# TensorE in tracing order in the stage of the last layer's first token group of a hybrid Conformer / RWKV-7 step

## The chip, the cores and the metric

The kernel runs on one core of a Trainium2 chip, as one launch. The metric is the device time of one execution in microseconds (us). The engines are called as the profile calls them: PE is TensorE's matmuls (PEld its weight loads), DVE is VectorE, ACT is ScalarE, POOL is GpSimd, SP is SyncE, which issues most DMAs.

## The reference

One inference step of a decoder of two layers with 1024 features, for a prompt of 1024 tokens (behind 16 learned meta tokens) and 8 single decode tokens, 1048 rows in all. Layer 0 mixes tokens with a causal Conformer convolution, layer 1 with RWKV-7; each is followed by a squared-ReLU MLP of width 4096. All is fp32. What matters here is the second half of layer 1:

```python
def _wkv7_step(S, inp):                       # per head, a 64x64 state
    r_t, w_t, k_t, v_t, kk_t, a_t = inp
    sa = einsum('bhvk,bhk->bhv', S, -kk_t)
    S = S * w_t + sa * (kk_t * a_t) + v_t * k_t
    return S, einsum('bhvk,bhk->bhv', S, r_t)
...
    yn = group_norm(y) * gn_g + gn_b          # per head, over 64 channels
    out = ((yn + bonus) * g) @ w_o            # "z" is (yn + bonus) * g
...
    h = h + out
    h = h + square(relu(rmsnorm(h) @ w_mlp_in)) @ w_mlp_out
```

## The kernel before

Every fp32 product of two big matrices is done as three fp32r matmuls: weights and activations are split into a rounded part (`_hi`) and a rest (`_lo`), and `mm3` (L187, L188, L189) adds hi·hi, lo·hi and hi·lo in PSUM. These are called **dense matmuls** below: 128x128 weights against 328 or 352 tokens. ACT casts the weights' hi part (L157), POOL subtracts for the lo part (L162), and DVE and ACT split the activations (L140, L141). `dense()` makes one 128-feature output tile of 24 dense matmuls and calls `fill()` in its middle, so that the work is cut into pieces of 12; `out` of the MLP calls `fill()` after every 6.

The rows are worked through in three token groups of 328, 352 and 352 for the output projection (`mixer_out`, tiles `ps_oo`, with eight inputs `zr` loaded from DRAM by SP at L1488 and split to `z_h`, `z_l`) and the MLP (`mlp`, tiles `ps_in` and `out`). The stage of this change is that of the first group. Before its start the projections of layer 1 (`p_v` the last of them, with `vt`, `nn` and `pk` behind them) have been done for all tokens.

Beside the dense work runs the recurrence, in 17 chunks of 64 tokens one after the other. `chunk()` is a generator. One chunk issues on PE: `A` (L1209, eight matmuls), `gg` (L1247), `bT` (L1270, eight transposes), `W` (L1277), `po` (L1247), `U` (L1293), `S` (L1302), `Y` (L1309 and L1312). A block of gg, po, W, U or S is 16 small matmuls on 32x32 or 64-wide parts of the array, one of Y 32; the trace has two records for each of these and for each matmul of A. Between them stand evictions on ACT and DVE, and each of them uses one of three PSUM banks (tag "w"). The last chunk's state goes out through `pfs` (L1330). At the stage's start the first twelve chunks are done. Two other streams run beside it: `decode_step` (L1368 to L1399, one step of the recurrence for the 8 decode tokens, `Sdec`) and `norm_gate`, which makes z for the later token groups, a half of the heads at a time: load of `ey`, mean and square, `yn` (four transposes on PE, L1429), `ez` (ACT, L1433), two DVE operations (L1435, L1436), a store to `d_z` by SP (L1437). The square `eq` (L1417) of the next half lies in the same buffer as `ez`, so it waits until that store has landed; behind it come L1422 to L1425 on DVE and ACT, and the next `yn`.

`filler()` deals these streams out over the stage's `fill()` calls, by the paces FA for the recurrence and NGA for decode and norm gates. This is the order of tracing. It isn't the order in which the engines run: the whole kernel is built under a scheduler that orders every engine's instructions from a timeline model of its own. So before the change the pieces of the three streams stand on PE where that planner puts them. Each engine then works its list strictly in order.

Lines of the stage: the `with` that is added stands round L1563 to L1566 (before). What follows is the stage of the second group.

Of the kernel before, what the change touches and what calls it, by code (L numbers as in the profile page):

```python
# [48 lines left out]
def hybrid_step(tc, x_prompt, x_sample, state_conv, state_shift, state_wkv, meta_tokens,  # L49
# [8 lines left out]
    nc = tc.nc  # L58
    ctx = ExitStack()
    with ctx:  # L60
# [77 lines left out]
        def split(hi, lo, src, eng_lo):  # L138

            nc.scalar.copy(hi, src)  # L140
            eng_lo.tensor_sub(lo, src, hi.bitcast(F32))  # L141
# [7 lines left out]
        def load_w(src, shape, name, eng_lo, tag="w", raw=None):  # L149

            a, b = shape
            if raw is None:
                raw = load_raw(src, shape, name)
            nb = cur["bufs"][tag]
            hi = cur["wsp"].tile([P, 8 * P], F32R, name=f"{name}_hi", tag=tag + "h", bufs=nb)
            lo = cur["wsp"].tile([P, 8 * P], F32R, name=f"{name}_lo", tag=tag + "l", bufs=nb)
            nc.scalar.copy(hi[:, :a * b], raw[:, :a * b])  # L157

            step = 2 * P if eng_lo is nc.gpsimd else a * b
            for c in range(0, a * b, step):  # L160
                cs = slice(c, min(c + step, a * b))
                eng_lo.tensor_sub(lo[:, cs], raw[:, cs], hi[:, cs].bitcast(F32))  # L162
            v = lambda t: t[:, :a * b].rearrange("p (a b) -> p a b", a=a)
            return v(hi), v(lo)
# [5 lines left out]
        def load_col(w, m, name, eng_lo, tag="w"):  # L170
            return load_w(col_src(w, m), (KT, P), name, eng_lo, tag)
# [13 lines left out]
        def mm3(ps, w, act, first, last):  # L185

            nc.tensor.matmul(ps, w[0], act[0], start=first, stop=False)  # L187
            nc.tensor.matmul(ps, w[1], act[0], start=False, stop=False)  # L188
            nc.tensor.matmul(ps, w[0], act[1], start=False, stop=last)  # L189

        def bank(name, tag="mm"):
            return cur[tag].tile([P, 512], F32, name=name, tag=tag)

        def dense(w, act, n, name, fill=None):
            ps = bank(f"ps_{name}")
            for k in range(KT):
                mm3(ps[:, :n], (w[0][:, k, :], w[1][:, k, :]), (act[0][:, k, :n], act[1][:, k, :n]), k == 0, k == KT - 1)
                if fill and k == KT // 2 - 1:
                    fill()
            return ps  # L200
# [5 lines left out]
        def tt(name, tag):  # L206
            return cur["tmp"].tile([P, cur["n"]], F32, name=name, tag=tag)
# [95 lines left out]
        def mlp(layer, groups, lag, eng_w, eng_h, fill=None, done=None):  # L303


            w_in, w_out = w_mlp_in[layer], w_mlp_out[layer]
            nj = DFF // P
            hid = {}

            def load_in(j):  # L310
                return load_col(w_in, j, f"wi{layer}_{groups[0][0]}_{j}", eng_w)

            def load_out(b):

                for i in range(2):
                    src = w_out[2 * b * P:(2 * b + 2) * P, i * 4 * P:(i + 1) * 4 * P].rearrange("(j p) c -> p j c", p=P)
                    yield load_w(src, (2, 4 * P), f"wo{layer}_{groups[0][0]}_{b}_{i}", eng_w)

            def inp(j, w, group):
                gn, hv, n, ah, al, rs, hid_pool = group  # L320
                if j % 2 == 0:
                    hid[gn, j // 2] = [hid_pool.tile([P, 2, cur["wide"]], F32R, name=f"h{q}{layer}{gn}_{j}", tag=f"h{q}") for q in "hl"]
                hh, hl = hid[gn, j // 2]
                ps = dense(w, (ah, al), n, f"in{layer}_{j}_{gn}", fill)
                with tc.high_priority(offset=HR):
                    r = tt(f"r{layer}_{j}_{gn}", "t1")
                    nc.vector.scalar_tensor_tensor(r[:, :n], ps[:, :n], 0.0, rs[:, :n], op0=ALU.max, op1=ALU.mult)  # L327
                    s = tt(f"s{layer}_{j}_{gn}", "t2")
                    nc.scalar.activation(s[:, :n], r[:, :n], AF.Square)  # L329
                    split(hh[:, j % 2, :n], hl[:, j % 2, :n], s[:, :n], eng_h)  # L330

            def out(b, i, w, group):
                gn, hv, n, ah, al, rs, hid_pool = group
                hh, hl = hid[gn, b]
                for m in range(4):
                    ps = bank(f"out{layer}_{b}_{gn}_{4 * i + m}")
                    for j in range(2):
                        mm3(ps[:, :n], [part[:, j, m * P:(m + 1) * P] for part in w], (hh[:, j, :n], hl[:, j, :n]), j == 0, j == 1)
                    with tc.high_priority(offset=HA):
                        nc.vector.tensor_add(hv[:, 4 * i + m, :], hv[:, 4 * i + m, :], ps[:, :n])  # L340
                    if fill:
                        fill()

            def outs(b):
                for i, w in enumerate(load_out(b)):
                    for group in groups:
                        out(b, i, w, group)

            last = nj - 1
            for j in range(last):  # L350
                w = load_in(j)
                for group in groups:
                    inp(j, w, group)
                b, odd = divmod(j - lag, 2)
                if b >= 0 and odd:
                    outs(b)
                if fill:
                    fill()
            for b in range((last - lag) // 2, nj // 2 - 1):
                outs(b)  # L360
            w, wo = load_in(last), list(load_out(nj // 2 - 1))
            for group in groups:
                inp(last, w, group)
                for i in range(2):
                    out(nj // 2 - 1, i, wo[i], group)
                if done and group is not groups[-1]:
                    done(group[0])

        with ExitStack() as l0:
# [6 lines left out]
            actp = [pool(l0, f"actp0{i}", 1) for i in range(2)]  # L376
            residp = [pool(l0, "resid00", 1)]
# [253 lines left out]
            with ExitStack() as s:  # L631
# [3 lines left out]
                fill, rest = filler(8 * KT, ([ranked(CV0, conv(0)), ranked(CV0, ln_silu(0))], EARLY * (15 * KT // 2 + 2 + 2 * MW + KT)))  # L635
# [43 lines left out]
            hidp = pool(l0, "hidp0", 2)  # L679
# [790 lines left out]
        with ExitStack() as l1:  # L1470
            open_weights(l1, 5, {"w": 5}, "f")
            open_tmp(l1, N2, "2", 3)
            residp = pool(l1, "resid1", 1)
            actp = pool(l1, "actp1", 1)
            hidp = pool(l1, "hidp1", 2)
# [5 lines left out]
            def mixer_out(g, residp, actp, fill, add):  # L1481
                lo, n = G2[g]
                h1 = hl[g] = residp.tile([P, KT, cur["wide"]], F32, name=f"h1_{g}", tag="h")
                nc.sync.dma_start(h1[:, :, :n], d_h[:, :, lo:lo + n])
                z = new_act(actp, f"z{g}", cur["wide"])
                for p in range(KT):
                    t = tt(f"zr{g}{p}", "t1")
                    nc.sync.dma_start(t[:, :n], d_z[:, p, lo:lo + n])  # L1488
                    split(z[0][:, p, :n], z[1][:, p, :n], t[:, :n], nc.vector)
                for m in range(KT):  # L1490
                    ps = dense(load_col(rwkv_w_o[0], m, f"wo{g}_{m}", nc.gpsimd), z, n, f"oo{g}_{m}", fill)
                    nc.vector.tensor_add(h1[:, m, :n], h1[:, m, :n], ps[:, :n])
                    add(m, h1[:, m, :n])
                    fill()
# [57 lines left out]
            def group(g, actp, hidp, sums):  # L1552
                n = G2[g][1]
                hv = hl[g][:, :, :n]
                return (g, hv, n, *mlp_in(actp, hv, n, 1, f"m1{g}", sums), hidp)
# [3 lines left out]
            fill, rest = filler(2 * KT + MLP_POINTS,  # L1559
                                ([until(NCH - 1)], FA * CHUNK_WAIT * (NCH - 1 - st["done"])),  # L1560
                                ([decode_step(), norm_gates(GN_OF[1]), ng2], NGA))
            add, sums = sums_of(0)
            mixer_out(0, residp, actp, fill, add)  # L1563
            mlp(1, [group(0, actp, hidp, sums)], 2, nc.gpsimd, nc.vector, fill)
            for _ in rest:
                pass  # L1566
            lw.close()
            outp = pool(l1, "outp", 1)
            cur["wide"] = max(n for lo, n in G2[1:])
# [2 lines left out]
            fill, rest = filler(2 * KT, ([ng2], NGB))  # L1572
            add, sums = sums_of(1)
# [6 lines left out]
            fill, rest = filler(2 * KT + MLP2_POINTS, ([ranked(FN, final(0))], FB))  # L1580
            add, sums = sums_of(2)
# [3 lines left out]
            def done(g):  # L1585
                end.append(filler(KT, ([final(g)], 24)))
# [38 lines left out]
```

## Time and profile before

| | |
|---|---|
| median of 3 runs | 2855.38 us (2850.13 to 2861.68) |
| span of the profiled execution | 2857.3 us |
| PE busy | 2677.4 us, 94% of the span |
| DVE, POOL, ACT busy | 69%, 60%, 47% |
| the stage | from the last projection (about 1837 us) to the second group's first `ps_oo` (2276.4 us) |
| the stage, PE and DVE busy | 413.65 us and 312.83 us of 440 |

The profiled execution has no time of its own beside its span of 2857.3 us; that lies 1.9 us over the median and within the three runs. PE is the engine that bounds the kernel nearly everywhere, and the profile's PE row says little about how well it is used: the ends of matmuls are modelled and overlap (a dense matmul of 328 columns has 0.31 us in the records and the next starts 0.15 us later). So in this stage the starts of matmuls are to be read, not their busy time.

### The profile page before, as it was taken

Reading aid. Unit: us, or ns where it says so; the run is one execution under the profiler, and the core shown is the slowest. Engines: PE = TensorE matmul, PEld = TensorE weight load, DVE = VectorE, ACT = ScalarE, POOL = GpSimd, SP = SyncE. Lnnn points to the kernel's source line nnn. Section 1 sums busy time; section 2 is a strip of 40 time slices with the busy share of each in tenths; the row PEclk is TensorE's granted clock in tenths of the full one; section 3 lists DMA queues with packets and bytes.
Section 4 is the critical chain, followed back from the end, with each engine's and each line's share of the span. In section 5 each row is a group of like instructions: output and inputs, shape, how many; then the busy total and the mean of one; then the engine's idle time right before and its main releaser. Section 6 shows DMA issues by size and latency. Waiting matters only on the chain. (4 is left out here: it accounts for less than half of the span.)

```text
span 2857.3 us, 54445 instructions
## 1 busy us (share of the span) xinstructions
PE 2677.4 (94%) x20554; PEld 2557.9 (90%) x20554; DVE 1958.0 (69%) x3726; ACT 1345.6 (47%) x2510; POOL 1703.4 (60%) x2295
## 2 busy tenths in 40 slices
PE   8999999999999899878788899979999999999998
PEld 7989999999999898867787788778889999999998
DVE  5999999995455545478896895689656764443444
ACT  5545444543454334565666857634445552222223
POOL 6676877887788775444543554646448783333332
PEclk9999999999999999988899999989999999999999
DMA  6662544454444642777777968856557742222211
GB/s 179 172 184 85 159 135 133 133 179 140 136 129 148 176 138 91 215 194 198 202 215 208 241 165 198 234 156 159 128 161 213 205 128 85 70 72 67 67 60 41
DMA packets 659285, 428.34 MB, mean 150 GB/s; under 512 B 126840, under 2 KB 609208, under 8 KB 659022
## 3 DMA queue, kind: packets, MB, share of 16 engines
q1 hardware_dynamic: 652780, 421.93, 52.6%
q8 instruction: 162, 2.65, 0.4%
q10 hardware_dynamic: 6018, 2.89, 0.4%
q14 instruction: 101, 0.83, 0.1%
q0 software_dynamic: 224, 0.03, 0.0%
HBM read 353.03 MB, written 72.66 MB: 149 GB/s over the span
## 5 line engine op out<-in xcount | busy, mean ns | idle before, releaser
L162 POOL TENSOR_TENSOR wo_lo<-wo_raw,wo_hi 128x256 fp32r<-128x256 f32 x736 | 561.5, 795 | 300.3 <-ACT wo_hi L157 265.5
L162 POOL TENSOR_TENSOR wi_lo<-wi_raw,wi_hi 128x256 fp32r<-128x256 f32 x640 | 490.4, 797 | 275.5 <-ACT wi_hi L157 264.1
L187 PE MATMUL out<-hh,wo_hi 128*128 128x352 f32 (+2 forms) x1536 | 503.5, 328 | 20.1 <-DVE h L340 10.6
L340 DVE TENSOR_TENSOR h<-h,out 128x352 f32<-128x352 f32 (+2 forms) x768 | 386.3, 510 | 197.8 <-PE out L189 196.9
L187 PE MATMUL ps_in<-m_h,wi_hi 128*128 128x352 f32 (+2 forms) x1536 | 497.4, 324 | 12.2 <-ACT m_h L269 11.5
L189 PE MATMUL out<-hl,wo_hi 128*128 128x352 f32 (+2 forms) x1536 | 496.0, 325 | 4.0 <-DVE hl L141 4.0
L188 PE MATMUL out<-hh,wo_lo 128*128 128x352 f32 (+2 forms) x1536 | 499.4, 325 | 0.0
L188 PE MATMUL ps_in<-m_h,wi_lo 128*128 128x352 f32 (+2 forms) x1536 | 496.5, 324 | 0.0
L189 PE MATMUL ps_in<-m_l,wi_hi 128*128 128x352 f32 (+2 forms) x1536 | 496.2, 323 | 0.1
L504 DVE SCALAR_TENSOR_TENSOR cv<-u,wdw,cv 128x352 f32<-128x352 f32 (+2 forms) x720 | 377.3, 575 | 0.7
L157 ACT CAST wi_hi<-wi_raw 128x1024 fp32r<-128x1024 f32 x160 | 168.1, 1050 | 396.9 <-PE out L189 188.4
L157 ACT CAST wo_hi<-wo_raw 128x1024 fp32r<-128x1024 f32 x184 | 192.9, 1049 | 316.8 <-PE out L189 145.6
L187 PEld LDWEIGHTS out<-hh,wo_hi 128*128 128x128 f32 x1536 | 292.6, 191 | 27.5 <-DVE h L340 14.8
L187 PEld LDWEIGHTS ps_in<-m_h,wi_hi 128*128 128x128 f32 x1536 | 290.6, 189 | 14.6 <-ACT m_h L269 11.6
L189 PEld LDWEIGHTS out<-hl,wo_hi 128*128 128x128 f32 x1536 | 291.6, 190 | 6.4 <-DVE hl L141 5.3
L188 PEld LDWEIGHTS out<-hh,wo_lo 128*128 128x128 f32 x1536 | 292.5, 190 | 1.7
L188 PEld LDWEIGHTS ps_in<-m_h,wi_lo 128*128 128x128 f32 x1536 | 290.3, 189 | 2.0
L189 PEld LDWEIGHTS ps_in<-m_l,wi_hi 128*128 128x128 f32 x1536 | 289.9, 189 | 1.9 <-DVE m_l L270 0.5
L327 DVE SCALAR_TENSOR_TENSOR r<-ps_in,rs_m 128x352 f32<-128x352 f32 (+2 forms) x192 | 98.6, 516 | 232.7 <-PE ps_in L189 228.9
L141 DVE TENSOR_TENSOR hl<-s,hh 128x352 fp32r<-128x352 f32 (+2 forms) x192 | 144.5, 754 | 109.9 <-ACT hh L140 109.8
L329 ACT ACTIVATE s<-r 128x352 f32<-128x352 f32 (+2 forms) x192 | 93.7, 490 | 130.8 <-DVE r L327 130.3
L162 POOL TENSOR_TENSOR wv_lo<-wv_raw,wv_hi 128x256 fp32r<-128x256 f32 x96 | 82.8, 892 | 24.1 <-ACT wv_hi L157 23.8
(402 smaller groups left out, 6155.5 us busy)
## 6 DMA issues: line engine op xcount, KB each, us to landing
wi_raw<-in_w_mlp_in_dram SPq DMA_DIRECT2D x160, 512.0 KB
wo_raw<-in_w_mlp_out_dram SPq DMA_DIRECT2D x160, 512.0 KB
wr_raw<-in_rwkv_w_r_dram SPq DMA_DIRECT2D x32, 512.0 KB
wk_raw<-in_rwkv_w_k_dram SPq DMA_DIRECT2D x32, 512.0 KB
wv_raw<-in_rwkv_w_v_dram SPq DMA_DIRECT2D x32, 512.0 KB
d_ab<-ab SPq DMA_DIRECT2D x32, 512.0 KB
pg_raw<-in_conv_w_pw_dram SPq DMA_DIRECT2D x24, 512.0 KB
pa_raw<-in_conv_w_pw_dram SPq DMA_DIRECT2D x24, 512.0 KB
```

Source lines behind the costliest of these rows:

```text
L141: eng_lo.tensor_sub(lo, src, hi.bitcast(F32))
L157: nc.scalar.copy(hi[:, :a * b], raw[:, :a * b])
L162: eng_lo.tensor_sub(lo[:, cs], raw[:, cs], hi[:, cs].bitcast(F32))
L187: nc.tensor.matmul(ps, w[0], act[0], start=first, stop=False)
L188: nc.tensor.matmul(ps, w[1], act[0], start=False, stop=False)
L189: nc.tensor.matmul(ps, w[0], act[1], start=False, stop=last)
L327: nc.vector.scalar_tensor_tensor(r[:, :n], ps[:, :n], 0.0, rs[:, :n], op0=ALU.max, op1=ALU.mult)
L329: nc.scalar.activation(s[:, :n], r[:, :n], AF.Square)
L340: nc.vector.tensor_add(hv[:, 4 * i + m, :], hv[:, 4 * i + m, :], ps[:, :n])
L504: nc.vector.scalar_tensor_tensor(acc[m][:, :n], ug[:, m, j:j + n], wdw[:, m, j:j + 1], acc[m][:, :n], op0=ALU.mult, op1=ALU.add)
```

## The change

The three calls of the stage and the drain of the rest are put into a context that takes PE's instructions there in the order of tracing. The other engines stay under the planner, which now plans them round that order of PE. No operation is added or left out.

```diff
             add, sums = sums_of(0)
-            mixer_out(0, residp, actp, fill, add)
-            mlp(1, [group(0, actp, hidp, sums)], 2, nc.gpsimd, nc.vector, fill)
-            for _ in rest:
-                pass
+            with tc.manual_schedule(engines={nc.tensor.engine}):
+                mixer_out(0, residp, actp, fill, add)
+                mlp(1, [group(0, actp, hidp, sums)], 2, nc.gpsimd, nc.vector, fill)
+                for _ in rest:
+                    pass
             lw.close()
```

The order of the instructions shows what this moves. First PE at the stage's start. Before, after the end of chunk 12's U, the output projection goes through four output tiles in turn, with one input z at a time:

```order
L1293 MATMUL U_22951<-w_22845,p_22742 64x64 x16
L187 MATMUL ps_oo_0_22587<-z_h,wo_0_hi 128x328
L188 MATMUL ps_oo_0_22587<-z_h,wo_0_lo 128x328
L187 MATMUL ps_oo_1_22709<-z_h,wo_1_hi 128x328
L188 MATMUL ps_oo_1_22709<-z_h,wo_1_lo 128x328
L187 MATMUL ps_oo_2_22792<-z_h,wo_2_hi 128x328
L188 MATMUL ps_oo_2_22792<-z_h,wo_2_lo 128x328
L187 MATMUL ps_oo_3_22893<-z_h,wo_3_hi 128x328
L188 MATMUL ps_oo_3_22893<-z_h,wo_3_lo 128x328
L189 MATMUL ps_oo_0_22587<-z_l,wo_0_hi 128x328
```

Now the last of the projections (`pk_7`) is followed at once by 12 matmuls of the first output tile, which need the first four inputs z, and only behind them stand S, Y and the rest of the chunk. The end of the 12, and what follows:

```order
L188 MATMUL ps_oo_0_22589<-z_h,wo_0_lo 128x328
L189 MATMUL ps_oo_0_22589<-z_l,wo_0_hi 128x328
L1302 MATMUL S_22602<-uv,bkt_21382 64x64 x16
L1309 MATMUL Y_22619<-sv,xa_12564 64x64 x16
L1312 MATMUL Y_22619<-uv,nr_21164 64x64 x16
L1209 MATMUL A_22660<-xa_12563,bk_21791 128x256 x2
L1209 MATMUL A_22668<-xa_12563,bk_21791 128x256 x2
L1368 MATMUL pdd_22681<-ident,ddec 48x128 x2
L187 MATMUL ps_oo_0_22589<-z_h,wo_0_hi 128x328
```

Chunk 12's S, Y, A, gg, bT, W, po and U stood ahead of the first `ps_oo` before, from S among the last projections on; now they all stand behind its first 12 matmuls.

Second, SP's issues ahead of the fourth input `zr` (the first three are issued earlier). Before:

```order
L1203 DMA vt_22881<-d_v 64x8x64 x2
L146 DMA wo_7_raw<-in_rwkv_w_o_dram 128x8x128
L146 DMA wi_0_0_raw<-in_w_mlp_in_dram 128x8x128
L1199 DMA p_23349<-d_p 128x8x32
L1163 DMA ni_23796<-d_n 128x1024
L146 DMA wi_0_1_raw<-in_w_mlp_in_dram 128x8x128
L1484 DMA h_0_22542<-d_h 128x8x328
L1387 DMA Sdec_23219<-in_state_wkv_dram 128x256
L1387 DMA Sdec_23372<-in_state_wkv_dram 128x256
L1488 DMA zr_22558<-d_z 128x328
```

Now:

```order
L146 DMA wo_5_raw<-in_rwkv_w_o_dram 128x8x128
L1034 DMA d_v<-vt_7_22467 128x2x128
L146 DMA wo_6_raw<-in_rwkv_w_o_dram 128x8x128
L1163 DMA ni_23798<-d_n 128x1024
L146 DMA wo_7_raw<-in_rwkv_w_o_dram 128x8x128
L1484 DMA h_0_22544<-d_h 128x8x328
L1387 DMA Sdec_23221<-in_state_wkv_dram 128x256
L146 DMA wi_0_0_raw<-in_w_mlp_in_dram 128x8x128
L1488 DMA zr_22560<-d_z 128x328
```

The chunk's own loads and stores (`xa`, `bk`, `vt`, `p`, `d_y`), one `wi` and one `Sdec` no longer stand ahead of the fourth `zr`.

Third, PE in the middle of the stage, where a gg of the recurrence meets `ps_in_7`. Before, they alternate, one row of each in turn:

```order
L189 MATMUL ps_in_6_0_24280<-m_l,wi_0_6_hi 128x328
L1247 MATMUL gg_24311<-x_24267,no_24179 32x32 x6
L187 MATMUL ps_in_7_0_24360<-m_h,wi_0_7_hi 128x328
L1247 MATMUL gg_24311<-x_24267,no_24179 32x32
L188 MATMUL ps_in_7_0_24360<-m_h,wi_0_7_lo 128x328
L1247 MATMUL gg_24311<-x_24267,no_24179 32x32
```

Now the block is whole:

```order
L189 MATMUL ps_in_6_0_24282<-m_l,wi_0_6_hi 128x328
L1247 MATMUL gg_24313<-x_24269,no_24181 32x32 x16
L1270 MATMUL bT_24341<-ident,bk_24176 128x128 x4
L1270 MATMUL bT_24347<-ident,bk_24176 128x128 x4
L187 MATMUL ps_in_7_0_24362<-m_h,wi_0_7_hi 128x328
```

A number such as x16 behind a row counts instructions that follow each other and read alike. Over the part of the stage from the first `ps_in` to `pfs`, PE changes 215 times between a dense matmul and another one before, and 58 times now (173 and 36 of them to or from a block of small matmuls). Behind `pfs`, the norm gates' `yn` stand 60, 60, 72, 60, 60, 72, 60, 60 and 72 dense matmuls apart, with 348 behind the last; before they stood 66, 121, 96, 83, 96, 96, 96, 96 and 88 apart, with 67 behind the last.

## The prediction

> **What bounds the kernel now.** I read the page's head and its slices first, then busy times by stretches of the stage, and last PE's timeline.
>
> ```profile
> span 2857.3 us, 54445 instructions
> PE 2677.4 (94%) x20554; PEld 2557.9 (90%) x20554; DVE 1958.0 (69%) x3726; ACT 1345.6 (47%) x2510; POOL 1703.4 (60%) x2295
> ...
> PE   8999999999999899878788899979999999999998
> ...
> PEclk9999999999999999988899999989999999999999
> ```
>
> PE is busy nearly throughout, so a gain must make PE's own list shorter, and a loss is a time in which PE has to stand. The span is the profiled execution's own time; the runs' median is 2855.38 us, 1.9 us less. I work on the span and carry the difference over. Slices 27 to 32 of the page are the stage, and the dip of PEclk lies at its start. I cut the stage at the first `ps_in` and at `pfs`, the end of the recurrence: A, B and C.
>
> ```profile
> 1837.00:1916.30 79.30, 59.00 (x589) 53.09 (x588) 55.72 (x116) 30.70 (x61) 45.02 (x56) 0.81 0.75 195
> 1916.30:2125.00 208.70, 206.84 (x2028) 172.89 (x2028) 155.03 (x344) 91.78 (x183) 101.96 (x125) 0.93 0.52 135
> 2125.00:2277.00 152.00, 147.81 (x970) 143.53 (x970) 102.09 (x184) 79.28 (x141) 120.22 (x148) 0.99 0.74 213
> ```
>
> Columns: window and length, then busy us of PE, PEld, DVE, ACT and POOL with counts, granted clock, DMA share, GB/s. A loses 20 us of PE's time to waits, at a clock of 0.81. B has PE busy all but 1.9 us, but the same view of `mm3`'s first line alone counts its dense matmuls:
>
> ```profile
> 1916.30:2125.00 208.70, 74.79 (x214) 43.22 (x214) 0.93 0.52 135
> ```
>
> Three times 214 are 642. What one takes is read from starts: undisturbed, and where small matmuls alternate with them.
>
> ```profile
> 2165.28 0.31 PE L187 MATMUL ps_in<-m_h,wi_hi 128*128 128x328 f32 x1
> 2165.43 0.31 PE L188 MATMUL ps_in<-m_h,wi_lo 128*128 128x328 f32 x1
> ...
> 1993.27 0.24 PE L1247 MATMUL gg<-x,no 32*32 32x32 f32 x2
> 1993.44 0.42 PE L188 MATMUL ps_in<-m_h,wi_lo 128*128 128x328 f32 x1
> 1993.79 0.24 PE L1247 MATMUL gg<-x,no 32*32 32x32 f32 x2
> ...
> 1963.97 1.15 PE L1277 MATMUL W<-sv,xa 128*64 128x64 f32 x32
> 1965.05 0.69 PE L1247 MATMUL po<-p,gg 32*32 32x32 f32 x32
> 1965.68 0.42 PE L187 MATMUL ps_in<-m_h,wi_hi 128*128 128x328 f32 x1
> ```
>
> A dense matmul takes 0.15 us. A whole block of 32 records takes 0.63 us (po), so two records take 0.04. A pair of one dense and one gg would be 0.19 us; alternating it takes 0.52 (1993.27 to 1993.79). So going over and back costs 0.33 us, one change 0.165 us. That is in no idle column, because the modelled ends cover it.
>
> **The change, part by part.**
>
> B, fewer changes. By the order, 215 changes become 58: 157 times 0.165 is **25.9 us less**. The Trainium skill, page "TensorEngine Tiling (Array Packing)", section "Key Properties", says that a change of the tiling mode, not one of the tile alone, drains TensorE. By that only the changes to and from blocks of small matmuls (173 to 36) would count, 22.6 us in place of 25.9; the rows here can't part the two.
>
> B's clock of 0.93 is 14.6 us of full clock missing over 208.7 us. The alternating stretches have part of it, and new waits will keep the rest: 5 us back, from 0 to 10. 42 dense matmuls (6.3 us) go from B to behind `pfs` (600 stay of 642), and W and po of one chunk come in from A (1.08 + 0.63 = 1.7 us).
>
> B, new waits. The planner put dense matmuls into each gap of the chain of a chunk. In the order of tracing, S, Y and four matmuls of A stand in a row, then 12 dense, then gg, bT, bT, all in three PSUM banks in turn. What a bank's eviction takes is seen where PE waited for one:
>
> ```profile
> 1865.40 1.03 PE L1209 MATMUL A<-xa,bk 128*128 128x256 f32 x4
> 1866.35 1.15 PE L1302 MATMUL S<-uv,bkt 128*64 128x64 f32 x32
> 1867.34 1.10 PE L1309 MATMUL Y<-sv,xa 128*64 128x64 f32 x32
> ...
> 1869.67 1.10 PE L1209 MATMUL A<-xa,bk 128*128 128x256 f32 x4 [1.01 <-DVE nr L1217]
> ```
>
> A was through at 1866.35, its bank free only at 1869.67: 3.3 us. In the new order, between the last A's end and the bT that needs its bank, lie 12 dense (1.8 us), gg and half of bT (1.0 us), and one A eviction stands before the other on DVE. I take 3 us a chunk, near that row, for seven chunks: **21 us**, from 1 us (the wait seen) to 6 us (two such evictions in a row). DVE is busy 155.03 of 208.7 us and gets the same work in less time, so a smaller price isn't likely. B: -25.9 - 5 - 6.3 + 1.7 + 21 = **-14.5 us**, from -34 (7 us of waits, 10 us of clock) to +11 (42 us, 0 of clock).
>
> A, the wait for z. These are PE's, ACT's and SP's rows:
>
> ```profile
> 1836.35 0.71 PE L1064 MATMUL pk<-rk,hsum 128*128 128x264 f32 x2
> ...
> 1856.49 0.64 PE L187 MATMUL ps_oo<-z_h,wo_hi 128*128 128x328 f32 x1 [4.78 <-ACT z_h L140]
> ...
> 1880.67 0.60 PE L1270 MATMUL bT<-ident,bk 128*128 128x128 f32 x4
> 1881.02 0.85 PE L189 MATMUL ps_oo<-z_l,wo_hi 128*128 128x328 f32 x4
> ...
> 1916.33 0.64 PE L187 MATMUL ps_in<-m_h,wi_hi 128*128 128x328 f32 x1 [11.51 <-ACT m_h L269]
> ```
>
> ```profile
> 1855.97 1.20 ACT L140 CAST z_h<-zr 128x328 fp32r<-128x328 f32 x3 [5.46 <-DMA bk<-d_ab]
> ...
> 1874.85 0.46 ACT L140 CAST z_h<-zr 128x328 fp32r<-128x328 f32 x1 [2.08 <-DMA zr<-d_z]
> ```
>
> ```profile
> 1864.95 1.61 SPq L1488 DMA_DIRECT2D zr<-d_z  x3
> ```
>
> Three inputs came at 1856, the fourth at 1874.85, and PE filled the time up to 1856 with chunk 12. Now the first 12 matmuls need the fourth, and chunk 12 is queued behind them on PE, its evictions behind that on ACT and DVE. SP's list ahead of the fourth `zr` loses some 2.3 MB, about 9 us at the 265 GB/s moved there:
>
> ```profile
> 1837.00:1857.00 20.00, 14.62 (x183) 11.60 (x183) 6.74 (x14) 10.90 (x22) 15.91 (x22) 0.70 1.02 265
> ```
>
> So the 12 begin about 1867 (1861 to 1875), after some 30 us without work. Behind them stand 192 dense (28.8 us), and of the recurrence S, Y, A, gg, bT, W, po, U, A, S, Y, A, gg, bT: by the rows above 1.0 for S, W or U, twice that for Y, 1.9 for four matmuls of A, 0.65 for gg or po, 0.7 for eight transposes (four in 0.35 at 1880.67), together 17 us. 22 changes are 3.6 us, chain waits 5 us (two bank waits of 1 and one of 3.3). The clock after the wait costs 3 us: the 20 us with a shorter wait had 0.70. Then the last `h`, its square, the sums and `st_m`, which now stands ahead of `ps_in`, 5 us of the 11.5 before. 1867 + 28.8 + 17 + 3.6 + 5 + 3 + 5 = 1929.4, **+13 us** on 1916.3; from -6 (1861, no chain wait, no clock loss, `st_m` hidden) to +29 (1875, and four chain waits of 3.3 us). A page speaks against such a wait too: the Trainium skill, "TensorE: Matmul & The Clock Gate", section "Part 1: The HAM clock gate", has the array at half rate after an idle window of 3.4 us until a busy one has passed. An estimate by that page is 1.7 us (half of one window) in place of my 3; the granted 0.70 agrees with a halved clock in part of that stretch.
>
> C, the norm gates. Their chain, in rows of PE, ACT and SP:
>
> ```profile
> 2175.41 0.49 PE L1429 MATMUL yn<-ident,ey 96*128 96x96 f32 x4
> 2188.54 0.60 PE L1429 MATMUL yn<-ident,ey 128*128 128x128 f32 x4
> 2204.67 0.60 PE L1429 MATMUL yn<-ident,ey 128*128 128x128 f32 x4
> ```
>
> ```profile
> 2179.04 0.37 SPq L1437 DMA_DIRECT2D d_z<-ez  x1
> ```
>
> ```profile
> 2184.39 0.63 ACT L1417 ACTIVATE eq<-ey 128x512 f32<-128x512 f32 x1 [1.67 <-DMA d_z<-ez]
> ```
>
> From yn to yn it was 13.1 and 16.1 us, and 5.35 us of the first lie between the store's issue and its landing (2179.04 to 2184.39), which nothing on PE shortens. The halves are serial through that buffer. Before, 96 dense matmuls (14.4 us) lay between, so PE reached yn when it was ready. Now 60 or 72 lie there: 9.0 or 10.8 us, with yn and two changes 9.9 or 11.7. PE will stand at each yn. I take 13.5 us a half, near the shorter row, since fewer evictions crowd DVE: 9 times 13.5, then 360 dense behind the last (348, and 12 of the next `oo`) at 54 us, together 175.5 us, **+23.5 us** on 152. At PE's own 9.9 and 11.7 it would be 148.5 (-3.5), at 16.1 199 (+47). The 6.3 us moved out of B are in these.
>
> **Sum:** 13 - 14.5 + 23.5 = +22 us. The span becomes 2879, the time 2877.4 us; behind the stage PE has no idle time to take it up.
>
> **The rivals.**
>
> Faster: the changes' price is all that moves. For it: 25.9 us are counted by rows, the clock may give 10, and the page's DVE at 69% has room. Against it: the bank's 3.3 us and yn's 13.1. The point is whether DVE and ACT release banks within some 2.8 us, and halves run in under 11.7 us; then B gives 34, A costs half of its 13 us, C nothing: 2855.4 - 34 + 6 = 2827 us.
>
> No change: the waits are only half as large (B -24, A +6, C +13): 2850 us, or DVE's load sets B's end and PE's shorter list just idles longer. For it: DVE's 155 us of 208.7.
>
> Slower still: each chain wait at its upper row (B +4, A +20, C +35): 2914 us. For it: 16.1 us stands beside 13.1; against: fewer interruptions on DVE. That the change does not do what it says is excluded by the order of PE.
>
> **How the numbers follow.** My forecast of about +22 us has a chance of 0.45, slower still 0.12, no change 0.23, faster 0.20. The predicted time is the forecast's, 2877 us. The forecast's own range is 2860 to 2897 (A and C within 10 us, B within 12). The range reaches from the faster case's neighbourhood, 2834, to 2908, which leaves out about 1 in 10 on each side. Half a percent, about what a measurement here can tell from no change, is 14 us: below 2841 0.20, above 2870 0.57, between them 0.23.
>
> **What would show it.** In the new profile: one-by-one alternation gone, and B's dense matmuls at 0.15 us outside the waits (else the 0.165 is wrong); a wait of some 30 us at the first `ps_oo`, ended by `z_l` or `z_h` of the fourth input near 1867 (else A); PE idle ahead of gg, bT or A released by DVE or ACT, about 3 us a chunk (else B); idle of 2 to 4 us before each of nine `yn`, released by DVE (else C). I am wrong if yn comes without a wait, or if the chain's waits sum to under 10 us in B.

## The result, and the profile after

No change that can be measured: 2853.97 us (median of 20 runs, 2848.91 to 2859.68) against 2855.11 us before (20 runs, 2847.36 to 2861.68), ratio 0.9993, 95% interval 0.9983 to 1.0003. The forecast was +22 us. The new profiled execution has a span of 2852.2 us, 5.1 us under that of before; the 20 runs of each kernel spread over 11 and 14 us, so the profiles are compared stage by stage.

The stage is cut where it was cut before, at the first `ps_in` (now 1920.6) and at `pfs` (now 2099.5); the second group's first `ps_oo` is at 2272.5. The new kernel, by windows; columns as before (length, busy us of PE, PEld, DVE, ACT, POOL, then granted clock, DMA share, GB/s):

```profile
1837.00:1920.50 83.50, 58.28 (x599) 52.82 (x600) 63.80 (x143) 35.03 (x71) 38.85 (x50) 0.81 0.70 186
1920.50:2099.50 179.00, 163.10 (x2042) 151.76 (x2042) 148.26 (x315) 85.71 (x174) 98.47 (x121) 0.97 0.56 147
2099.50:2273.00 173.50, 156.31 (x1013) 153.86 (x1014) 104.07 (x187) 80.84 (x142) 118.06 (x151) 0.95 0.65 191
```

B took 178.9 us in place of 208.5, **29.6 us less**. C took 173.0 in place of 151.5, **21.4 us more**. For A the common point is the last `pb` pair but one, the last that both orders have at the same place, at 1818.8 before and 1817.9 now: from there to the first `ps_in` it took 97.6 and 102.8 us, **5.2 us more**. Together 3.0 us less, with 0.9 us from an earlier start: 3.9 of the 5.1 us. So the change moved much, and what B won was given back in A and C.

B, a gg in the new kernel's PE timeline. It is one block of 32 records, and the dense matmuls beside it start 0.15 us apart:

```profile
1997.47 0.32 PE L188 MATMUL ps_in<-m_h,wi_lo 128*128 128x328 f32 x1
1997.63 0.31 PE L189 MATMUL ps_in<-m_l,wi_hi 128*128 128x328 f32 x1
1997.87 0.69 PE L1247 MATMUL gg<-x,no 32*32 32x32 f32 x32
1998.49 1.09 PE L1270 MATMUL bT<-ident,bk 128*128 128x128 f32 x8
1999.34 0.40 PE L187 MATMUL ps_in<-m_h,wi_hi 128*128 128x328 f32 x1
```

What PE waited for in B now (line, releaser: us in all, times, longest):

```profile
PE gg L1247 <- ACT no L1215: 3.5, 3, 1.3
PE Y L1309 <- DVE nr L1217: 3.0, 2, 1.6
...
PE out L187 <- DVE r L327: 2.5, 1, 2.5
PE bT L1270 <- DVE nr L1217: 2.0, 5, 0.9
PE S L1302 <- ACT uv L1295: 1.7, 1, 1.7
PE A L1209 <- DVE nr L1217: 1.6, 1, 1.6
PE U L1293 <- DVE w L1279: 0.9, 1, 0.9
```

The new waits stand where they were looked for, at the evictions of A (`no`, `nr`), of U (`uv`) and of W (`w`): 12.7 us in these rows, the longest 1.7. The `out` row is the MLP's own, and the row left out (`st_m`, 2.9 us) ends before the first `ps_in`. In all PE's busy column leaves 15.9 us idle in B, 14 more than before.

A, the two waits for z in the new kernel, in rows of PE, ACT and SP:

```profile
1844.47 0.64 PE L187 MATMUL ps_oo<-z_h,wo_hi 128*128 128x328 f32 x1 [14.46 <-ACT z_h L140]
1856.47 0.64 PE L187 MATMUL ps_oo<-z_h,wo_hi 128*128 128x328 f32 x1 [8.35 <-ACT z_h L140]
```

```profile
1843.96 1.19 ACT L140 CAST z_h<-zr 128x328 fp32r<-128x328 f32 x3
1855.96 1.38 ACT L140 CAST z_h<-zr 128x328 fp32r<-128x328 f32 x3 [10.80 <-DMA zr<-d_z]
```

```profile
1831.95 0.46 SPq L1488 DMA_DIRECT2D zr<-d_z  x1
...
1848.91 2.43 SPq L1488 DMA_DIRECT2D zr<-d_z  x3
```

The fourth input came at 1856, 19 us earlier than before, and the 12 matmuls started at 1844 and went on at 1856; the prediction had them begin at 1867. The three inputs behind the third were issued at 1848.91, where it had been 1864.95. Of these 16 us, 9 lie ahead of the third input: its own issue came at 1831.95, and before at 1840.92:

```profile
1840.92 0.53 SPq L1488 DMA_DIRECT2D zr<-d_z  x1
```

The other 7 us are SP's list between the two issues, 17.0 us in place of 24.0.

C, some of the `yn` in the new kernel's PE timeline, and behind them the DVE operation that ends the chain:

```profile
2100.60 0.66 PE L1429 MATMUL yn<-ident,ey 128*128 128x128 f32 x4
2113.19 0.63 PE L1429 MATMUL yn<-ident,ey 128*128 128x128 f32 x4 [2.87 <-ACT hh L140]
2128.33 0.88 PE L1429 MATMUL yn<-ident,ey 96*128 96x96 f32 x4 [3.93 <-issue]
...
2192.52 1.11 PE L1429 MATMUL yn<-ident,ey 128*128 128x128 f32 x4 [3.12 <-DVE ey L1425]
...
2215.00 0.55 PE L1429 MATMUL yn<-ident,ey 96*128 96x96 f32 x4
```

```profile
2112.22 0.88 DVE L1425 TENSOR_TENSOR ey<-ey,ems 128x512 f32<-128x512 f32 x1
2127.37 0.86 DVE L1425 TENSOR_TENSOR ey<-ey,ems 96x512 f32<-96x512 f32 x1
```

Two of the waits are put down to `hh` and to "issue", but the multiplication of `ey` ends at 2113.10 and 2128.23, 0.1 us before each of these yn, so it is taken for the releaser there too. The waits at yn are 15.0 us in all, at six of the nine yn behind the first; at the other three PE didn't wait. Nine halves took 114.4 us, 12.7 each.

### The profile page after: what moved, and what is told of

Same layout as the page of the kernel before. It is cut to its first block, busy times and chain, and to the rows that moved or that the text cites. A ratio compares the mean times of both kernels' runs of the same rounds, so it can differ in the third digit from the quotient of the medians.

```text
span 2852.2 us, 54462 instructions
## 1 busy us (share of the span) xinstructions
PE 2638.4 (93%) x20554; PEld 2545.3 (89%) x20554; DVE 1954.7 (69%) x3726; ACT 1346.6 (47%) x2510; POOL 1700.7 (60%) x2295
## 4 chain that ended last, share of the span: by engine, by line
PE 31%; DVE 11%; DMA 4%; ACT 2%; issue 2%; POOL 1%; SPq 0%; DVEq 0%; ACTq 0%; POOLq 0%
PE out L187 4%; PE out L188 4%; PE out L189 4%; PE ps_in L187 4%; PE ps_in L189 4%; PE ps_in L188 4%; DVE tt L1168 1%; PE ps_oo L187 1%; DVE ni L1169 1%; PE ps_oo L189 1%; PE ps_oo L188 1%; PE A L1209 1%; DMA d_z<-ez 1%; DVE mx L813 1%; DVE xa L1216 1%
## 5 line engine op out<-in xcount | busy, mean ns | idle before, releaser
L140 ACT CAST hh<-s 128x352 fp32r<-128x352 f32 (+2 forms) x192 | 92.1, 482 | 5.7
```

## The experiments

Two theories stand against each other. **Blocks and yn:** B wins because small and dense matmuls no longer alternate; C loses because yn are dealt out faster than their chain. **Rival 1:** another engine sets the end of the stage, whatever PE's order. **Rival 2:** C loses by the MLP's own waits in the order of tracing. All ratios are to the kernel before, run beside the experiment on the same chip (medians of 2859 to 2861 us there), with 95% intervals; a gain or loss in us beside a ratio is worked out from that ratio, and twins are compared by their medians. A and C of a kernel are read from its one profile.

### The order of tracing until the recurrence's end only

```diff
+ms = ExitStack()
+ms.enter_context(tc.manual_schedule(engines={nc.tensor.engine}))
+def fill_ms():
+    fill()
+    if st["done"] >= NCH - 1:
+        ms.close()
+mixer_out(0, residp, actp, fill_ms, add)
+mlp(1, [group(0, actp, hidp, sums)], 2, nc.gpsimd, nc.vector, fill_ms)
```

> TensorE takes the order of tracing only until the recurrence has ended; behind it (part C) the planner orders it again. Theory (blocks and yn): the change wins some 30 us between the first ps_in and pfs (part B), because small matmuls no longer alternate with dense ones, and gives it back because the norm gates' yn stand only 60 to 72 dense matmuls apart in part C. With yn 85 to 107 apart again, C costs what it cost before plus the 42 dense moved into it: A +4, B -30, C +6 and less for pfs, together about -20 us, 2835 us, ratio 0.993. Rival 1 (another engine sets the stage's end): no change, 2855 us, within 0.3%. Rival 2 (the waits of C are the MLP's own, hh and hl, in a C that begins earlier): C keeps half or more of its +21, 2845 us or more.

Measured: 2833.26 us, ratio **0.9914** (0.9900 to 0.9928), 25 us less. Part C of this kernel:

```profile
2093.25:2246.40 153.15, 148.72 (x1008) 146.23 (x1009) 103.28 (x186) 80.36 (x142) 126.15 (x154) 1.00 0.74 215
```

153 us in place of 173, at full clock, with the same number of dense matmuls behind `pfs`. Rival 1 falls: the time follows PE's order. Rival 2 falls in the form that it has here, since C keeps 2 us of its 21; whether the MLP's own order of tracing costs is left to the runs below. B was 178.3 us, as in the change.

### The same, from the MLP's start on

The context is entered behind `mixer_out` in place of ahead of it.

> The order of tracing only from the MLP's start until the recurrence has ended, so the output projection (part A) is the planner's again. Theory: part A is as before (no wait of 14 and 8 us at the first ps_oo), B wins 26 to 30 us, C as in the kernel with the order until pfs: about -25 us, 2830 us, ratio 0.991, some 4 us better than that one. Rival 1: no change, 2855 us. If part A's new waits cost nothing on balance, it is the same as the one with the order until pfs.

Measured: 2835.87 us, ratio 0.9922 (0.9905 to 0.9938). It isn't the 4 us better that were expected; the two intervals overlap. In its profile A took 99.6 us from the `pb` pair, 103.2 in the kernel above, but B 183.4 in place of 178.3. What the planner's order saves in A it loses again in B, with 2 us more of idle time on PE and a clock of 0.96 in place of 0.98; why isn't shown.

### The order of tracing behind the recurrence only

The context is entered when the recurrence has ended and closed behind the drain of the rest; A and B are the planner's.

> The order of tracing only from the recurrence's end on (part C): yn 60 or 72 dense matmuls apart as in the change, A and B as before. Theory: +15 us (21 less the 42 dense that the change had moved there), 2870 us, ratio 1.005; PE idle before most yn. Rival 1: no change, since then the stage's end isn't PE's. Rival 2: the same loss, but with PE waiting for hh and hl and not at yn.

Measured: 2882.22 us, ratio **1.0080** (1.0064 to 1.0096), 23 us slower where 15 were expected. PE's waits in part C (178.7 us, before 151.5):

```profile
PE yn L1429 <- DVE ey L1425: 15.0, 6, 5.2
PE yn L1429 <- issue: 6.7, 2, 3.6
PE out L187 <- ACT hh L140: 1.6, 1, 1.6
```

21.7 us at yn and 2 us at the MLP's own `hh` and `hl`: against rival 2. The expectation had left out the clock, which was 0.93 in C in place of 0.99, some 10 us of full clock.

### Slower gates through the whole stage

```diff
-            NGA, NGB, FA, FB = 262.15, 45.48, 1.57, 40
+            NGA, NGB, FA, FB = 215, 45.48, 1.57, 40
```

> The change with the norm gates' and the decode step's pace lowered from 262.15 to 215, so that after pfs yn stand 60 to 90 (mean 77) dense matmuls apart and the last has 84 behind it instead of 348. Theory: A +4, B -25 to -30, and in C a half takes 12.5 us of PE's work against a chain of 13: C +6 (moved dense work), +5 for the chain and the three more yn behind pfs: about -15 us, 2840 us, ratio 0.995. Rival 1: no change. Rival 2: C loses as much as in the change, 2854 us.

Measured: 2854.94 us, ratio 0.9978 (0.9969 to 0.9987): 6 us, not 15. The slower pace also moves the first two yn from the recurrence to behind `pfs`. The first and the last of the twelve in its profile:

```profile
2098.30 0.66 PE L1429 MATMUL yn<-ident,ey 128*128 128x128 f32 x4
...
2251.24 0.78 PE L1429 MATMUL yn<-ident,ey 96*128 96x96 f32 x4 [3.63 <-DVE ey L1425]
```

Eleven halves of 13.9 us are 153 us. C took 173.2 us, as long as in the change, which is what rival 2 of this run forecast. PE still stood at six of the yn, 11.9 us in all, and the clock was 0.96. I had counted dense matmuls per half and had forgotten the number of halves: with twelve yn behind `pfs` the chain lasts nearly through C, and little dense work is left behind the last.

### Slower gates behind the recurrence only

```diff
+def later(gen):
+    for wait in gen:
+        yield wait * (1.4 if st["done"] >= NCH - 1 else 1)
...
-([decode_step(), norm_gates(GN_OF[1]), ng2], NGA))
+([decode_step(), later(norm_gates(GN_OF[1])), later(ng2)], NGA))
```

> The change, the order of tracing through the whole stage, with one edit: behind the recurrence's end the norm gates' pace is lowered by 1.4, so that the ten yn there stand 78 to 96 dense matmuls apart (mean 88) and the last has 132 behind it, close to what the planner chose in the kernel with the order until pfs (85 to 107, 137). Up to pfs the two orders of TensorE are the same as in the change. Theory (what part C loses in the change is the yn being dealt out faster than their chain of 13 to 14 us): the waits at yn go, part C takes 153 to 157 us in place of 173, 2835 us, ratio 0.993. Rival 2 (the tracing order of the MLP itself costs in part C, whatever the yn do): part C stays over 165 us, 2845 us or more.

Measured: 2837.86 us, ratio **0.9924** (0.9911 to 0.9938). Part C took 159.9 us, and PE's waits at yn were 2.5 us:

```profile
PE yn L1429 <- DVE ey L1425: 2.5, 2, 2.0
PE out L187 <- ACT hh L140: 1.6, 1, 1.6
```

So with the whole stage in the order of tracing, the pace of one stream behind `pfs` is worth 13 us of C's 21. C missed the 153 to 157 us that were expected. Of the 6.7 us to the 153.2 of the planner's C, some 3 are the clock, 0.98 in place of 1.00, and some 3 are PE's idle time (7.4 us in place of 4.4). What lowered the clock isn't shown.

### A shorter chain of the norm gate

```diff
-nc.vector.tensor_add(z[:, :w], z[:, :w], bv[:, :w])
-nc.vector.tensor_mul(z[:, :w], z[:, :w], gt[:, :w])
-nc.sync.dma_start(d_z[:, ps_, lo:lo + n], fm(z))
+nc.vector.tensor_add(y[:, :w], z[:, :w], bv[:, :w])
+nc.vector.tensor_mul(y[:, :w], y[:, :w], gt[:, :w])
+nc.sync.dma_start(d_z[:, ps_, lo:lo + n], fm(y))
```

In the change:

> The change, with one edit in the norm gate: the sums and products behind yn go into the tile of ey (two buffers) in place of ez, so that the next half's square needs only to wait for the addition and no longer until the store to d_z has landed. The order of TensorE is the change's, yn 60 to 72 dense matmuls apart. Theory (in part C the yn wait for the chain through that buffer, 13 to 14 us a half): without the 5 us of the store the chain is under 9.9 us, PE's waits at yn go, and part C falls from 173 us to about 150: 2833 us, ratio 0.992. Rival 2 (the waits of C are the MLP's own, or the clock's): part C stays within 5 us of 173, 2850 us.

With the order of tracing until the recurrence's end:

> The order of tracing until the recurrence's end, and the short gate chain. With theory: part C was 153 us with the planner's own spacing and had hardly a wait at yn, so the shorter chain gives nothing more there: 2833 us, ratio 0.991, the same as with the order until pfs alone. If it is 5 us or more under that one, the chain still cost something there.

In the kernel before:

> The kernel before (planner's order everywhere) with the short gate chain alone. Theory: before, PE waited 4 us in part C and none of it at yn, so nothing is to be won: 2855 us, ratio 1.000. If it is faster by 10 us or more, the short chain is a gain by itself and the other kernel's gain with it says nothing about the order of TensorE.

Measured: 2857.80 us, ratio 0.9995 (0.9981 to 1.0008); 2851.62 us, 0.9978 (0.9962 to 0.9993); 2876.20 us, 1.0061 (1.0041 to 1.0081). All three missed. The edit costs 0.6% by itself, and most of that lies ahead of the stage, where the norm gates and the buffers of `ey` change too: in the last kernel's profile the `pb` pair comes 13 us later than before, and in the stage A is 11 us shorter, B 10 longer (218.5 us) and C 4 longer. In the first kernel the pair comes 10 us later than in the change, and C takes 165.9 us, 7 less; PE waited at yn once, for 5.3 us. So the shorter chain took most of the waits at yn away, but C fell by 7 us and not by 23: the theory of this run holds in part. Read against each other, with the edit in both, the order of tracing through the whole stage is worth 0.9995 / 1.0061 = 0.9934, 19 us, where it was worth nothing without it. C is still 10 us longer by the order (21 without the edit). As A and B differ too, this is support and no proof.

### The price of a change

Four kernels with the planner's order of before, and 12 extra matmuls in the second half of each of the 64 `ps_in` tiles of the last two groups; within these halves PE follows the order of tracing in all four. They write to a bank that nothing reads. In the alternating kernels one stands behind each dense matmul, in the block kernels all 12 stand behind the 12; those on the whole array have the full identity as weights.

```diff
+def small():
+    nc.tensor.matmul(spare[32:64, :32], ident[:32, :32], ident[:32, :32], start=True, stop=True, tile_position=(0, 32))
+def whole():
+    nc.tensor.matmul(spare[:, :32], ident, ident[:, :32], start=True, stop=True)
```

> The kernel before with 12 extra matmuls (32 columns, on one 32x32 part of the array, fp32, into a bank that nothing reads) in the second half of each of the 64 ps_in tiles of the last two token groups, one behind each dense matmul; the order of TensorE within these halves is that of tracing. It is to be compared with its twin, which has the same 12 in one block behind the 12 dense ones. Theory (a change between a dense and a small matmul costs 0.165 us, by the pairs read before): 22 changes more a tile than the twin, 64 tiles, 232 us more than the twin. Rival (the alternation costs little, and what was read as its price was waits or a low clock): within 40 us of the twin.

> The twin: the same 768 extra small matmuls, 12 in one block behind the 12 dense matmuls of a half tile. Theory: 64 blocks of 12 (24 records of 0.02 us each, 0.5 us) with two changes each, 0.8 us a block: about 53 us more than before, 2908 us.

> As the alternating kernel of small matmuls, but the extra matmul uses the whole array (128x128 identity as weights, 32 columns, fp32), so that the tiling of the array never changes. If the price belongs to a change of the array's tiling, this one is hardly slower than its twin (under 40 us). If it belongs to any change from fp32r to fp32 weights, it is as much slower than its twin as the small ones, some 230 us.

> The twin of the full-array one: the same 768 extra matmuls in blocks of 12 behind 12 dense ones. Expected between 40 and 100 us more than before, by how long an fp32 matmul of 32 columns with its own weight load takes.

Measured: small, alternating 3327.60 us (1.1635, 1.1598 to 1.1673), in a block 2931.86 us (1.0256, 1.0222 to 1.0290): **396 us** between the twins, where 232 were expected. Whole array, alternating 3031.30 us (1.0596, 1.0559 to 1.0633), in a block 3026.89 us (1.0591, 1.0551 to 1.0631): 4 us. The block kernels cost 73 and 168 us on before, where 53 and 40 to 100 were expected: an extra matmul on the whole array takes 0.22 us in either arrangement. The price belongs to the change of the array's tiling (the profile's 128\*128 and 32\*32), not to the change of weights or of type. These twins alone don't exclude that alternation hides some of the 0.22 us and so a price. The profile of before speaks against it. Where its clock was 0.50 (1955 to 1961), dense matmuls alternate with gg, 0.81 us a pair, and then with the transposes bT, which use the whole array, 0.49 us a pair.

```profile
1955.70 0.31 PE L1247 MATMUL gg<-x,no 32*32 32x32 f32 x2
1955.94 0.64 PE L188 MATMUL out<-hh,wo_lo 128*128 128x328 f32 x1
1956.51 0.31 PE L1247 MATMUL gg<-x,no 32*32 32x32 f32 x2
...
1959.45 0.41 PE L1270 MATMUL bT<-ident,bk 128*128 128x128 f32 x1
1959.52 0.62 PE L189 MATMUL out<-hl,wo_hi 128*128 128x328 f32 x1
1959.94 0.41 PE L1270 MATMUL bT<-ident,bk 128*128 128x128 f32 x1
```

Twice the 0.15 us of a dense matmul and the 0.09 of a bT at full clock are 0.48, so the pair with bT pays next to nothing. The alternating kernel of small matmuls at full and at half clock:

```profile
2810.14 0.43 PE L188 MATMUL ps_in<-m_h,wi_lo 128*128 128x352 f32 x1
2810.51 0.24 PE L199 MATMUL spare_in<-ident 32*32 32x32 f32 x2
2810.68 0.43 PE L188 MATMUL ps_in<-m_l,wi_hi 128*128 128x352 f32 x1
...
2801.38 0.31 PE L199 MATMUL spare_in<-ident 32*32 32x32 f32 x2
2801.62 0.66 PE L188 MATMUL ps_in<-m_h,wi_hi 128*128 128x352 f32 x1
2802.22 0.31 PE L199 MATMUL spare_in<-ident 32*32 32x32 f32 x2
```

A pair takes 0.54 us at 2810 and 0.84 us at 2801. A dense matmul of 352 columns takes 0.16 and two small records 0.04, so one change is 0.17 us at full clock, as the prediction read it. By the twins it is 396 us / (22 x 64) = 0.28 us. The clock explains the rest: over this stage of the alternating kernel (2357 to 3301) its mean was 0.76, so 48% of 944 us went at half clock. As an estimate, 0.30 of each 0.84 us there is lost, some 160 us; with 1408 changes of 0.17 us, 239 us, that is 399. A stretch of the stage in the alternating kernel, and one in its twin:

```profile
2800.00:2900.00 100.00, 100.00 (x464) 76.10 (x464) 17.82 (x33) 13.15 (x21) 14.79 (x21) 0.74 0.10 32
```

```profile
2480.00:2580.00 100.00, 100.00 (x816) 97.12 (x814) 37.14 (x70) 22.09 (x33) 32.44 (x44) 1.00 0.20 63
```

## Why the prediction was wrong

**What bounds.** Right. The edits of PE's order moved the time, from 25 us less to 23 us more.

**B, changes: the price right, the count wrong.** 0.165 us was confirmed at 0.17. The prediction counted changes between dense and other matmuls, 157 fewer. By the twins, and by the rows at 1955 to 1960, changes between dense matmuls and A or bT cost next to nothing, and those between A, bT or yn (whole array) and U, Y or gg (parts of it) have to be counted. In the orders of before and now, changes between whole-array and small blocks in B are 173 + 50 and 36 + 9: 178 fewer, 29.4 us in place of 25.9. The Trainium skill, page "TensorEngine Tiling (Array Packing)", section "Key Properties", says that a change of the tiling mode, not one of the tile alone, drains TensorE. The twins agree: 396 us with such changes, 4 us without. The prediction named this rule but left out the changes that the dense matmuls have no part in (22.6 us), and it held that the rows of before can't part the two counts; those at 1955 to 1960 do.

**B, clock: mis-sized.** 0.93 became 0.97: missing clock of 14.6 us became 5.4, 9.2 us back and not 5, within the stated 0 to 10. The twins show that alternation alone lowers the clock, to 0.74 over 100 us with no idle time on PE. In the profile of before all four stretches at half clock that begin in B (at 1954, 1999, 2012 and 2077) begin within about 6 us of the start of an alternation with gg.

**B, new waits: the step that failed most.** The prediction took the time that one bank was seen taken, 3.3 us, of which PE had waited 1.0, as about the wait of every chunk, and seven chunks: 21 us. Both factors were too large. B's trace has 80 records of A and 192 of U, five and six chunks, and the chain's waits were 12.7 us, some 2.3 a chunk and never over 1.7 at once; with the MLP's own, B's new waits were 14. Why most banks came free in time isn't shown: DVE was busier than before (148.26 of 179.0 us, 83%), as the prediction had said. With the terms as now counted and measured: -29.4 - 9.2 - 6.3 + 1.7 + 14 = -29.2 us, measured -29.6, predicted -14.5. The agreement to 0.4 us is in part luck. The first term is a count times a price, and as the other engines were planned anew in each kernel, no run moves PE's order alone.

**A: mechanism right, size wrong.** PE did stand for z, 22.8 us in two waits, and it cost 5.2 us, not 13. The step that failed is the start at 1867: of the 16 us by which the issue moved, the prediction had the 7 on SP's list behind the third input (9 by its estimate), and had the 9 us by which that input was itself issued earlier at nothing.

**C: right.** Predicted +23.5, measured +21.4. The halves took 12.7 us, near the shorter row, not 13.5, and PE stood at six of nine yn, not at each. Two things were not in the sum, and they partly cancel. The clock fell from 0.99 to 0.95, 7 us of full clock, beside 13 us more idle time on PE. Against that, `pfs` was whole now, where it had alternated with dense matmuls before: 21 changes between the whole array and parts of it in C's trace became 1, some 3 us at the price above.

**The sum.** A and B were each too dear, by 8 and 15 us, in the same direction: 22 us became -3. The rival "no change" named the half-sized waits, and its A (+6) came true. Its total, 2850 us, lies close to the measured time, but in part by luck: B gained 6 us more than its -24, and C lost 8 us more than its +13.

## What to carry to other kernels

Count the changes between matmuls on the whole array and on parts of it when an order is judged, since the profile's idle columns don't show them. In B, keeping the small blocks whole was worth some 38 us with the clock, and the gaps that alternation had filled cost 14. Before a stream is put into a fixed order, compare the time of one step of its serial chain (here 12.7 us) with the engine's work between two steps (here 9.9 or 11.7 us), and multiply the chain by the number of its steps: where it is longer, the engine stands. Here the order of tracing until the recurrence's end is worth 0.9% (2833 us), the lowest ratio of all kernels run; the intervals of the one from the MLP's start and of the one with slower gates behind the recurrence overlap with it.

## What the hardware showed unexpectedly

The granted clock fell to 0.74 over 100 us in which PE was busy the whole time, when dense and 32x32 matmuls alternated, and it stayed at 1.00 in the twin with whole-array matmuls at the same alternation:

```profile
2700.00:2800.00 100.00, 100.00 (x703) 100.00 (x701) 30.36 (x55) 18.81 (x29) 26.72 (x36) 1.00 0.16 48
```

The granted clock of a few us is either 0.50 or 1.00 in these traces, and values between are means. In the alternating kernel it is 0.50 from 2803 to 2808, without any wait, and 1.00 from 2810 to 2813.2.

The clock fell also about waits of PE of only 2 to 4 us: 0.90 over the first 50 us of part C in the new kernel, with two waits of 2.9 and 3.9 us.

```profile
2099.50:2149.50 50.00, 43.18 (x286) 42.64 (x287) 27.63 (x51) 21.77 (x41) 29.07 (x37) 0.90 0.76 224
```

At these and at the later ones of 2.2 and 3.1 us a stretch at half clock begins (at 2113.7, 2127.4, 2178.6 and 2192.2); at those of 1.4 and 1.5 us none does.
